# A decoder layer on one core: late gate products 8 chunks later, scatters tied to V blocks, V lists mixed, the branch ahead of the residual

## The chip, the cores and the metric

The kernel runs on one core of a Trainium2 chip. Its engines are named as in the profile: PE (matmuls; PEld are its weight loads), DVE, ACT, POOL and SP; POOL and SP also issue DMAs. The metric is the device time of one execution in microseconds, as the median of several runs. A profiled execution is one execution more, with its own time.

## The reference

One layer of an autoregressive decoder for 256 tokens of 2048 numbers, all in float32: two kinds of attention, an attention into 256 memory tokens, and then a retrieval of experts (PEER), then a last RMSNorm. The change touches only the retrieval and the last norm:

```python
def peer_ffn(hn, w_pq, sub_keys, u_tab, v_tab):          # 8 heads, 16 experts a head, 16384 experts
    q = (xt @ w_pq).reshape(T, PEER_HEADS, 2, PEER_D_KEY // 2)
    s = jnp.einsum('thpd,hpkd->thpk', q, sub_keys)
    top_s, top_i = lax.top_k(s, K)
    ...
    expert = ia * PEER_N_KEYS + ib
    gate = jax.nn.softmax(best_s, axis=-1)
    ...
        a = jnp.einsum('td,ted->te', xb, u_tab[eb])
        hidden = gb.astype(xb.dtype) * jax.nn.gelu(a)
        return jnp.einsum('te,ted->td', hidden, v_tab[eb])
...
h = h + peer_ffn(rmsnorm(h, norm_ffn), ...)
y = rmsnorm(h)
```

## The kernel before

The kernel does not gather rows of U per token. It multiplies the hidden state with the whole of U, 128 chunks of 128 experts each (`u_chunk`), and keeps for each chunk a tile of 128 experts x 256 tokens in one of 16 buffers `hb` of 8 chunks each: 8 in the pool `ba` (chunks 0 to 63), 8 in the pool `bb` (chunks 64 to 127). What no token chose is multiplied by a gate of zero. Then only experts that some token chose are taken further to V.

**Splitting.** Each float32 operand that comes from memory is split in two: `parts` (L66) makes `hi` on ACT (L69) and the remainder `lo` on DVE (L71), in three buffers each; PE multiplies both. A U chunk is two loads of 512 KB (`raw`, SP's queue, four buffers), two splits, 16 matmuls at L79 and 16 at L81 per half. `raw` buffers are also used for late gates and, later, for listed rows.

**Gates.** While the top-k search runs (pieces popped one per chunk), each chosen place gets its gate by an indirect DMA from POOL into a table in DRAM (`put_gate`, L922; 256 of them, four popped per step; `puts`). When all puts have landed, the table is read back. Chunks from `first` on have their gates in their `hb` buffer before their products (eight reads of 1 MB, L730 `hb<-table`). Chunks before `first` were already computed without a gate; groups of four of them are done late (`early`, `done`): one read of 0.5 MB into a `raw` buffer (L730 `gates<-table`), one product on DVE (L702), and a reduction of the largest values (`peaks`, L753). `end` is the chunk at which the last put is popped; reads of late gates begin at `end + 6`.

**Lists.** `lists(part, ...)` (L771) ranks the experts in use and gives each a row in DRAM. There are two parts, experts of chunks 0 to 87 and of 88 to 127, and three classes in each: experts wanted by tokens of the first half only (class 0), of the second half only (class 1), or of both (class 2). One indirect DMA per chunk (L811, "scatter", POOL) writes its rows to their places: 88 in part 0, 40 in part 1. The scatters of part 1 are closures in `late`.

**V blocks.** `plan` cuts the classes into blocks of 128 rows, 22, 22 and 17 in part 0 and 10, 10 and 8 in part 1, 89 blocks in all, and writes their order (`seq`) and the ends of four stretches (`ends`). `block(i)` fetches 128 rows of V for block i + 11 (`fetch`, L963, indirect DMA on POOL, 1 MB, into an `hb` buffer of `ba` or `bb` by the pattern `homes`), reads the listed rows of the block (SP, L1016, up to four blocks at a time into a `raw` buffer), splits the hidden values (`hh` L1003, `hl` L1005) and the V rows, and adds 12 matmuls (24 for class 2) to the four PSUM banks of the token half (L991, L993, L995). `run(n)` does the blocks up to the end of stretch n, and may pop one of `late` per block. `bank(tb)` takes the four PSUM banks of a token half: the second half's only after the first stretch, when the planner's PSUM (`cps`) has been given back.

The order before: stretch 0 is all 22 blocks of class 0 of part 0; stretch 1 mixes classes 1 and 2 of part 0 (39 blocks); stretch 2 classes 0 and 2 of part 1 (18); stretch 3 class 1 of part 1 (10). Between stretch 1 and stretch 2 the residual is added by matmuls with a unit matrix (L1071), and then comes a branch (`rest`, L1132) for experts that found no place; with these inputs its body is skipped. After stretch 2 the first token half is complete, after stretch 3 the second; squares (L1085), products with the gain (L1105, L1123), scaling and stores follow.

**What sets the order.** The framework schedules each engine's instructions ahead of time from a simulated timeline, by priority and readiness, so the order on an engine need not be that of the code; on the chip each engine then runs its list in that order and waits on semaphores. Nothing passes the branch in either direction.

Of the kernel before, what the change touches and what calls it, by code (L numbers as in the profile page):

```python
# [18 lines left out]
F32 = mybir.dt.float32  # L19
F32R = mybir.dt.float32r  # L20
U32 = mybir.dt.uint32
SYNC = mybir.DependencyInfo(mybir.DependencyClass.Sync, mybir.DependencyReason.DATA)
AF = mybir.ActivationFunctionType
ALU = mybir.AluOpType
# [12 lines left out]
GROUP = 8  # L37
# [5 lines left out]
CAPS = ((22, 22, 17), (10, 10, 8))  # L43
# [7 lines left out]
class Layer:  # L51
# [14 lines left out]
    def parts(self, raw, eng=None):  # L66
        nc = self.nc
        hi = self.st.tile([128, HALF], F32R, tag="hi", name="hi", bufs=HI)
        nc.scalar.activation(hi, raw, AF.Copy)  # L69
        lo = self.st.tile([128, HALF], F32R, tag="lo", name="lo", bufs=LO)  # L70
        (eng or nc.vector).tensor_tensor(out=lo, in0=raw, in1=hi.bitcast(F32), op=ALU.subtract)  # L71
        return hi, lo


# [544 lines left out]
    def peer(self):  # L619
        nc, tc, a = self.nc, self.tc, self.a  # L620
        with ExitStack() as es:
# [14 lines left out]
            def some(n):  # L636
                for _ in range(n):
                    if puts:
                        puts.pop(0)()

            with ExitStack() as e2:
                ps = self.ps = e2.enter_context(tc.tile_pool(name="ups", bufs=2, reuse_waits="tile", space=bass.MemoryType.PSUM))
                pieces = []
                with tc.tile_pool(name="tk", bufs=1, reuse_waits="tile") as tk:
# [22 lines left out]
                    c = 0  # L667
# [14 lines left out]
                self.plan()  # L682

                end = c + (len(puts) + 3) // 4
                first = (end + 10 + GROUP - 1) // GROUP * GROUP
                early = list(range(0, first, 4))
                done = {}
                part = 0
                late = []
                while c < 128:  # L690
                    if c % GROUP == 3 and c + 5 >= first and c + 5 < 128:
                        self.table_read(self.buf[(c + 5) // GROUP][:, :, :T], c + 5)
                    if c >= end + 6 and early:
                        g = early.pop(0)
                        t = self.st.tile([128, 4 * W], F32, tag="raw", name="gates", bufs=RAW)
                        t = t[:, :4 * T].rearrange("p (i t) -> p i t", t=T)
                        self.table_read(t, g)
                        done.setdefault(c + 1, []).append((g, t))
                    self.u_chunk(c, c >= first)
                    for g, t in done.pop(c, []):  # L700
                        d = self.buf[g // GROUP][:, g % GROUP:g % GROUP + 4, :T]
                        nc.vector.tensor_mul(d, d, t)  # L702
                        self.peaks(g, g + 4)
                    some(4)
                    if c >= first and (c % 4 == 3 or c >= 124):
                        self.peaks(c if c >= 124 else c - 3, c + 1)
                    c += 1
                    if part == 0 and c >= PARTS[0][1] and not early and not done:
                        late = self.lists(0, ps, "sc", 2)
                        part = 1  # L710
                    if part == 1 and not late and not self.sets:
                        for k in range(11):
                            self.fetch(k)
                    for _ in range(4):
                        if late:
                            late.pop(0)()
# [54 lines left out]
    def lists(self, part, pool, tag, bufs):  # L771


        nc, tc, cl = self.nc, self.tc, self.cl
        lo, hi = PARTS[part]
        n = hi - lo
        v = nc.vector
        cap, base = CAPS[part], BASE[part]
        t = lambda tag, k=2: cl.tile([128, k, n], F32, tag=tag, name=tag)
        f = t("f")  # L780
        v.tensor_scalar(f, self.peak[:, :, lo:hi], 0.0, None, op0=ALU.not_equal)
        both = t("both", 1)
        v.tensor_mul(both[:, 0], f[:, 0], f[:, 1])
        v.tensor_sub(f[:, 0], f[:, 0], both[:, 0])
        v.tensor_sub(f[:, 1], f[:, 1], both[:, 0])
        p = self.ranks(f, n, 2, pool, tag, bufs)
        ok = t("ok")
        for j in range(2):
            v.scalar_tensor_tensor(ok[:, j], p[:, j, :n], float(cap[j] * 128), f[:, j], op0=ALU.is_lt, op1=ALU.mult)
        v.tensor_sub(f, f, ok)  # L790
        for j in range(2):
            v.scalar_tensor_tensor(ok[:, j], p[:, j, :n], float(base[j] - BIG), ok[:, j], op0=ALU.add, op1=ALU.mult)
        for j in range(2):
            v.tensor_add(both[:, 0], both[:, 0], f[:, j])
        p = self.ranks(both, n, 1, pool, tag, bufs)

        limit = float(cap[2] * 128)
        x = t("x", 1)
        v.tensor_scalar(x[:, 0], p[:, 0, :n], limit, ROWS[part] - limit - base[2], op0=ALU.is_ge, op1=ALU.mult)
        v.scalar_tensor_tensor(x[:, 0], p[:, 0, :n], float(base[2] - BIG), x[:, 0], op0=ALU.add, op1=ALU.add)  # L800
        v.tensor_mul(x[:, 0], x[:, 0], both[:, 0])
        for j in range(2):
            v.tensor_add(x[:, 0], x[:, 0], ok[:, j])
        v.tensor_scalar(x[:, 0], x[:, 0], float(BIG), None, op0=ALU.add)
        where = cl.tile([128, n], U32, tag="where", name="where")
        v.tensor_copy(where, x[:, 0])  # L806

        v.tensor_reduce(out=self.over[:, part:part + 1], in_=both[:, 0], axis=AX.X, op=ALU.add)

        def write(i):  # L810
            ins = nc.gpsimd.indirect_dma_start(  # L811
                out=self.rows[part], out_offset=bass.IndirectOffsetOnAxis(ap=where[:, i - lo:i - lo + 1], axis=0),
                in_=self.buf[i // GROUP][:, i % GROUP, :], in_offset=None,
                bounds_check=ROWS[part] + n * 128 - 1, oob_is_err=False)

            tc.declare_no_dep(ins.ins, group="rows%d" % part, reason="rows of their own")
            tc.add_to_no_dep_group("rows%d" % part, ins.ins)
            self.written[part].append(ins)

        return [(lambda i=i: write(i)) for i in range(lo, hi)]  # L820

    def topk_pieces(self, h, tb, pq, sk):
# [108 lines left out]
    def plan(self):  # L931

        self.seq, self.ends, self.sets, self.index = [], [], {}, {}
        self.homes = ([self.ba] * 8 + [self.bb] * 3 + [self.ba] * 8 + [self.bb] * 5) * 4
        for lists in (((0, 0),), ((0, 1), (0, 2)), ((1, 0), (1, 2)), ((1, 1),)):
            todo = []
            for part, cls in lists:
                n = CAPS[part][cls]
                todo += [((k + 0.5) / n, part, cls, k) for k in range(n)]
            self.seq += [x[1:] for x in sorted(todo)]  # L940
            self.ends.append(len(self.seq))

# [26 lines left out]
    def v_phase(self):  # L969
        nc, tc, a = self.nc, self.tc, self.a  # L970
# [5 lines left out]
        with ExitStack() as es:  # L976
            psum = lambda n: tc.tile_pool(name=n, bufs=1, reuse_waits="tile", space=bass.MemoryType.PSUM)
            out = []
# [43 lines left out]
            def block(i):  # L1022
                part, cls, k = self.seq[i]
                if i + 11 < len(self.seq):
                    self.fetch(i + 11)
                raw = self.sets.pop(i)
                listed = load(part, cls, k)
                tbs = (cls,) if cls < 2 else (0, 1)
                for tb in tbs:
                    left[tb] -= 1  # L1030
                h = hidden_pair(listed[:, :T] if cls == 2 else listed[:, cls * 128:(cls + 1) * 128])
                for hf in range(2):
                    vh, vl = self.parts(raw[:, hf * HALF:(hf + 1) * HALF])
                    for tb in tbs:
                        tq = slice(tb * 128, (tb + 1) * 128) if cls == 2 else slice(0, 128)
                        products(tb, hf, [x[:, tq] for x in h], vh, vl, left[tb] == 0)

            at = [0]

            def run(upto, beside=[], after=0):  # L1040


                first = at[0]
                while at[0] < self.ends[upto]:
                    if at[0] - first >= after and beside:
                        beside.pop(0)()
                    block(at[0])
                    at[0] += 1

            bank(0)  # L1050
            with psum("cps") as cps:
                late = self.lists(1, cps, "sc", 2)
# [9 lines left out]
                nc.vector.tensor_copy(self.flag, flag)  # L1062
            nc.gpsimd.dma_start(res, self.hres)
            nc.gpsimd.dma_start(gain, a["norm_final"].partition_broadcast(128))
            run(0, late, 4)
            bank(1)
            run(1, late)

            for tb in range(2):
                for k in range(KD):  # L1070
                    mm(out[tb][k // 4][:, k % 4 * 128:(k % 4 + 1) * 128], res[:, k, tb * 128:(tb + 1) * 128],  # L1071
                       self.ident, start=False, stop=False)
            self.rest(hidden_pair, products)
            run(2)

            one = vw.tile([128, 1], F32, tag="fy", name="one", bufs=2)
# [182 lines left out]
```

## Time and profile before

| | us |
|---|---|
| median of 3 runs | 1842.82 (1840.57 to 1849.99) |
| profiled execution, whole | 1836.41 |
| its span | 1834.6 |
| PE busy / PEld / DVE / ACT / POOL | 1695.8 / 1439.1 / 1272.7 / 961.6 / 760.3 |
| mean granted clock of PE | 0.97 |

The span runs from the first to the last instruction on record; the whole time has 1.8 us around it. Matmuls overlap, so PE's busy time says when PE was not idle rather than how much of its peak was used. In lists of waits the columns are the total, the number and the longest; in the timeline a start, a duration, the engine, and in brackets the idle time before it with what ended it; a duration with `x8` covers eight instructions in a row.

### The profile page before, as it was taken

To read this page: it belongs to the slowest core of one execution; us is meant where nothing else is said; L and a number is where in the kernel's file an instruction comes from. 1 tells how busy PE (TensorE), PEld (TensorE's weight loads), DVE (VectorE), ACT (ScalarE), POOL (GpSimd) and SP (SyncE) were. 2 spreads that over 40 slices of the span, in tenths; PEclk is the share of its full clock that TensorE was granted. 3 is DMA by queue.
4 is the path that set the end of the run, shared out by engine and by line. 5 is a ranking of instruction groups with operands and counts; after the bars stand their busy time and mean duration, and the time that the engine had idled before them with its cause. 6 is when DMAs were issued, how large, how long until landed. Compare 5 with 4: busy or idle time off the path is not lost. (4 is left out here: it accounts for less than half of the span.)

```text
span 1834.6 us, 25771 instructions
## 1 busy us (share of the span) xinstructions
PE 1695.8 (92%) x9056; PEld 1439.1 (78%) x9056; DVE 1272.7 (69%) x2304; ACT 961.6 (52%) x1441; POOL 760.3 (41%) x642
## 2 busy tenths in 40 slices
PE   8899999999999979999997299999999895999897
PEld 6788777887888868888886188888887774888785
DVE  6834575546678999999963299777665793666467
ACT  6534556764565446556543044544443573555356
POOL 5400000112132788888877200004774167744220
PEclk9999999999999989999999599999999997999999
DMA  7566344889846545666663788657888879797551
GB/s 278 170 231 202 134 141 152 317 315 373 277 151 196 174 121 173 184 186 187 192 196 105 247 269 269 205 187 213 253 250 308 319 293 359 299 414 271 203 189 71
DMA packets 127178, 416.30 MB, mean 227 GB/s; under 512 B 38041, under 2 KB 39817, under 8 KB 113344
## 3 DMA queue, kind: packets, MB, share of 16 engines
q1 hardware_dynamic: 88352, 254.34, 42.6%
q0 software_dynamic: 38688, 160.23, 23.9%
q8 instruction: 73, 1.20, 0.3%
q14 instruction: 65, 0.53, 0.1%
HBM read 370.50 MB, written 49.78 MB: 229 GB/s over the span
## 5 line engine op out<-in xcount | busy, mean ns | idle before, releaser
L71 DVE TENSOR_TENSOR lo<-raw,hi 128x1024 fp32r<-128x1024 f32 x436 | 538.3, 1237 | 249.4 <-ACT hi L69 228.6
L69 ACT ACTIVATE hi<-raw 128x1024 fp32r<-128x1024 f32 x440 | 464.5, 1058 | 458.1 <-PE acc L79 208.3
L79 PE MATMUL acc<-pair_f,hi 128*128 128x512 f32 x2304 | 584.7, 396 | 21.9 <-ACT hi L69 8.0
L79 PEld LDWEIGHTS acc<-pair_f,hi 128*128 128x128 f32 x2304 | 418.0, 190 | 100.8 <-ACT hi L69 10.8
L922 POOL DMA_INDIRECT table<-total,place x256 | 339.9, 1328 | 107.9 <-issue 75.2
L81 PEld LDWEIGHTS acc<-pair_f,lo 128*128 128x128 f32 x2304 | 316.7, 192 | 73.4 <-DVE lo L71 51.3
L81 PE MATMUL acc<-pair_f,lo 128*128 128x256 f32 x2304 | 325.2, 284 | 49.4 <-DVE lo L71 49.4
L71 DVE TENSOR_TENSOR lo<-vrows,hi 128x1024 fp32r<-128x1024 f32 x178 | 216.1, 1224 | 120.8 <-ACT hi L69 114.0
L69 ACT ACTIVATE hi<-vrows 128x1024 fp32r<-128x1024 f32 x178 | 186.0, 1059 | 148.2 <-PE out L993 91.1
L963 POOL DMA_INDIRECT vrows<-V,index x89 | 131.7, 1480 | 209.0 <-DVE lo L71 181.7
L811 POOL DMA_INDIRECT rows<-hb,where x128 | 142.3, 1112 | 164.0 <-DVE where L806 125.3
L991 PE MATMUL out<-hi,hh 128*128 128x512 f32 x456 | 140.5, 406 | 29.0 <-ACT hi L69 20.4
L993 PE MATMUL out<-hi,hl 128*128 128x512 f32 x456 | 144.2, 401 | 0.0
L995 PE MATMUL out<-lo,hh 128*128 128x512 f32 x456 | 140.0, 398 | 0.0
L79 PE MATMUL acc<-pair_x,hi 128*128 128x512 f32 x512 | 132.4, 397 | 0.0
L991 PEld LDWEIGHTS out<-hi,hh 128*128 128x128 f32 x456 | 87.0, 193 | 51.0 <-ACT hi L69 21.3
L79 PEld LDWEIGHTS acc<-pair_x,hi 128*128 128x128 f32 x512 | 91.8, 190 | 17.2 <-issue 1.4
L993 PEld LDWEIGHTS out<-hi,hl 128*128 128x128 f32 x456 | 87.1, 191 | 21.4 <-DVE hl L1005 0.2
L995 PEld LDWEIGHTS out<-lo,hh 128*128 128x128 f32 x456 | 86.3, 190 | 20.9
L81 PEld LDWEIGHTS acc<-pair_x,lo 128*128 128x128 f32 x512 | 70.9, 191 | 7.9 <-DVE lo L71 1.9
L81 PE MATMUL acc<-pair_x,lo 128*128 128x256 f32 x512 | 75.2, 286 | 1.5 <-DVE lo L71 1.5
L79 PE MATMUL acc<-pair_o,hi 128*128 128x512 f32 x256 | 66.3, 400 | 5.3 <-ACT hi L69 4.3
(376 smaller groups left out, 1879.1 us busy)
## 6 DMA issues: line engine op xcount, KB each, us to landing
raw<-U SPq DMA_DIRECT2D x256, 512.0 KB, 4.4
raw<-w_sb SPq DMA_DIRECT2D x32, 512.0 KB, 3.4
table<-zero POOLq DMA_DIRECT2D x16, 1024.0 KB, 4.4
raw<-w_out SPq DMA_DIRECT2D x32, 512.0 KB, 6.6
raw<-w_pq SPq DMA_DIRECT2D x32, 512.0 KB, 3.8
rows<-zero POOLq DMA_DIRECT2D x12, 903.0 KB, 9.1
listed<-rows SPq DMA_DIRECT2D x20, 516.0 KB, 4.5
raw<-w_kv SPq DMA_DIRECT2D x16, 512.0 KB, 3.3
```

The lines of the kernel that those rows point to most:

```text
L69: nc.scalar.activation(hi, raw, AF.Copy)
L71: (eng or nc.vector).tensor_tensor(out=lo, in0=raw, in1=hi.bitcast(F32), op=ALU.subtract)
L79: mm(ps, hi[:, n * m:(n + 1) * m], pair[:, k, :], start=first and n == 0, stop=False)
L81: mm(ps[:, T:], lo[:, n * m:(n + 1) * m], pair[:, k, :T], start=False, stop=last and n == len(ks) - 1)
L811: ins = nc.gpsimd.indirect_dma_start(out=self.rows[part], out_offset=bass.IndirectOffsetOnAxis(ap=where[:, i - lo:i - lo + 1], axis=0), in ...
L922: ins = self.nc.gpsimd.indirect_dma_start(out=self.table, out_offset=bass.IndirectOffsetOnAxis(ap=self.place[tb][:, s:s + 1], axis=0), in_ ...
L963: nc.gpsimd.indirect_dma_start(out=raw, out_offset=None, in_=self.a["V"], in_offset=bass.IndirectOffsetOnAxis(ap=self.index[part, cls][:, ...
L991: mm(out[tb][hf * 2 + q], hh, vh[:, q * 512:(q + 1) * 512], start=first, stop=False)
L993: mm(out[tb][hf * 2 + q], hl, vh[:, q * 512:(q + 1) * 512], start=False, stop=False)
L995: ins = mm(out[tb][hf * 2 + q], hh, vl[:, q * 512:(q + 1) * 512], start=False, stop=last)
```

## The change

It consists of five edits.

1. In `peer`: reads of late gates begin at `end + 14` instead of `end + 6`, and `first` is computed from `end + 18` instead of `end + 10`.
2. In `v_phase`: each scatter of part 1 gets a dependency on the last `lo` of the block just written (`self.last_lo`), and is popped after the block instead of before it; the count starts from block 3 instead of 4.
3. In `plan`: stretch 0 is 11 blocks of class 0; stretch 1 mixes the other 11 with classes 1 and 2 (50 blocks); stretch 2 mixes classes 0 and 2 of part 1 with the first 6 of class 1 (24 blocks); stretch 3 is the last 4 of class 1.
4. `bank(1)` thereby comes after 11 blocks.
5. `rest` (the branch) stands ahead of the residual matmuls.

```diff
@@ parts
-        (eng or nc.vector).tensor_tensor(out=lo, ...)
+        self.last_lo = (eng or nc.vector).tensor_tensor(out=lo, ...)
@@ peer
-                first = (end + 10 + GROUP - 1) // GROUP * GROUP
+                first = (end + 18 + GROUP - 1) // GROUP * GROUP
...
-                    if c >= end + 6 and early:
+                    if c >= end + 14 and early:
@@ lists, write(i)
+            return ins
@@ plan
-        for lists in (((0, 0),), ((0, 1), (0, 2)), ((1, 0), (1, 2)), ((1, 1),)):
+        a0, a1, a2 = CAPS[0]
+        b0, b1, b2 = CAPS[1]
+        for lists in (((0, 0, 0, 11),), ((0, 0, 11, a0), (0, 1, 0, a1), (0, 2, 0, a2)),
+                      ((1, 0, 0, b0), (1, 1, 0, b1 - 4), (1, 2, 0, b2)), ((1, 1, b1 - 4, b1),)):
             todo = []
-            for part, cls in lists:
-                n = CAPS[part][cls]
-                todo += [((k + 0.5) / n, part, cls, k) for k in range(n)]
+            for part, cls, lo, hi in lists:
+                todo += [((k + 0.5 - lo) / (hi - lo), part, cls, k) for k in range(lo, hi)]
@@ v_phase, run
                 while at[0] < self.ends[upto]:
+                    block(at[0])
                     if at[0] - first >= after and beside:
-                        beside.pop(0)()
-                    block(at[0])
+                        ins = beside.pop(0)()
+                        tc.add_manual_dep(ins.ins, self.last_lo.ins.name, SYNC, reason="one per block")
                     at[0] += 1
@@ v_phase
-            run(0, late, 4)
+            run(0, late, 3)
             bank(1)
             run(1, late)
+            self.rest(hidden_pair, products)
             for tb in range(2):
                 ... (the residual matmuls)
-            self.rest(hidden_pair, products)
             run(2)
```

More of the change, by code (lines that the diff above doesn't have):

```diff
@@ L70, in parts @@
         lo = self.st.tile([128, HALF], F32R, tag="lo", name="lo", bufs=LO)
-        (eng or nc.vector).tensor_tensor(out=lo, in0=raw, in1=hi.bitcast(F32), op=ALU.subtract)
+        self.last_lo = (eng or nc.vector).tensor_tensor(out=lo, in0=raw, in1=hi.bitcast(F32), op=ALU.subtract)
         return hi, lo
```

## The prediction

> **What bounds the kernel now.** I read first the page (engines and the span in 40 slices), then PE's waits, then the stages in windows, then the timeline around each stop. TensorE is busy 92% of the span, so time can only come from PE's stops; the waits say where they are.
>
> ```profile
> span 1834.6 us, 25771 instructions
> PE   8899999999999979999997299999999895999897
> PEclk9999999999999989999999599999999997999999
> PE acc L81 <- DVE lo L71: 50.8, 4, 48.2
> PE out L991 <- ACT hi L69: 20.4, 2, 14.8
> PE out L991 <- ACT hh L1003: 7.8, 2, 7.1
> ```
>
> The reader is to see two hollows in PE's row (a 2 near slice 23, a 5 near slice 33) and three waits: one of 48.2 us in the U chunks, 20.4 us in two pieces in the V blocks, one of 7.1 us at the branch. Call them A, B and C. All other PE waits are each under 15 us in total and in code that the change leaves alone.
>
> **A, the late gates.**
>
> ```profile
> 985.28 1.11 PE L81 MATMUL acc<-pair_f,lo 128*128 128x256 f32 x8
> 990.87 1.12 PE L81 MATMUL acc<-pair_f,lo 128*128 128x256 f32 x8
> 994.61 2.00 PE L79 MATMUL acc<-pair_f,hi 128*128 128x512 f32 x8
> 1010.87 0.98 POOL L922 DMA_INDIRECT table<-total,place  x1 [0.30 <-issue]
> 1014.13 7.27 POOL L730 DMA_DIRECT2D hb<-table  x8 [2.29 <-issue]
> 1021.39 0.56 POOL L730 DMA_DIRECT2D gates<-table  x1
> 1042.40 1.23 DVE L702 TENSOR_TENSOR hb<-hb,gates 128x1024 f32<-128x1024 f32 x1 [54.55 <-DMA gates<-table]
> 1044.82 2.08 PE L81 MATMUL acc<-pair_f,lo 128*128 128x256 f32 x8 [48.20 <-DVE lo L71]
> 1030.00:1035.00 5.00, 0.00 (x0) 0.00 (x0) 0.00 (x0) 0.00 (x0) 0.00 (x0) 0.50 1.02 351
> 1390.00:1440.00 50.00, 44.87 (x247) 38.04 (x246) 25.18 (x35) 18.55 (x28) 13.33 (x11) 1.00 0.99 397
> ```
>
> (In windows: span, the five engines' busy times, PE's clock, DMA share, GB/s.) One U chunk takes PE 990.87 - 985.28 = 5.59 us. DVE reaches the first late product at 1042.40 - 54.55 = 987.85 and stands; behind it in DVE's order are the splits that feed PE, which runs dry 8.8 us later (994.61 + 2.00 = 996.6). The product waits for a 0.5 MB read that POOL issues at 1021.4, behind its last gate put (1010.9) and eight 1 MB reads; the DMA then moves 351 GB/s and nothing else wants it.
>
> The change puts the product 8 chunks later, 8 x 5.59 = 44.7 us. In numbers of the code: 34 chunks run with the top-k pieces and 72 puts are left, so end = 52, reads start at chunk 66 instead of 58, `first` goes from 64 to 72, the late groups from 16 to 18, the 1 MB reads from 8 to 7. POOL's puts do not wait for DVE there (0.30 us of issue between them), so the reads still start at 1014. What changes is that U loads run beside them: 1.05 MB per 5.59 us is 188 GB/s. The nearest row of such sharing is 1390 to 1440 (V rows beside U loads): 397 GB/s, PE 44.87 of 50, so U got 169 of its 188. From 1014 to 1032.6 U takes 169 and the table reads 351 - 169 = 182 GB/s, 3.4 MB of their 7.9 (7 x 1.05 + 0.52). DVE, 1.9 us late from that sharing, stands at 1034.5; SP still fills four slots (2.1 MB); 4.5 + 2.1 MB at 351 GB/s take 19 us from 1032.6, but the fill is shared, so I put the product at about 1046 to 1051, take 1048. PE resumes 2.4 us after the product (as 1044.82 after 1042.40), at 1050.4, and would have stopped at 1034.5 + 8.8 = 1043.3: about 7 us idle, and 1.9 us of slower chunks. A is worth 48.2 - 7 - 1.9 = 39 us. Bounds: 48 if the reads have landed; and with U at its full 188 GB/s to the end, 7.9 MB at 351 - 188 = 163 GB/s land at 1062, PE idles from 1041 to 1065, worth 25. A loss would need the product after 1042.4 + 44.7 = 1087, excluded by these rates.
>
> The Trainium skill (DMA: Bandwidth & Descriptors, section Queues, rings and completion order) says that each DMA engine goes round robin between queues, a packet at a time. By that the U loads, with 4 KB runs against the table's 1 KB, would lose nothing and the table reads would be the slow ones: the 1.9 us go, the product comes later, and A would be worth about 37; the row of 1390 to 1440, where PE does lose 10% beside larger runs, is no contradiction and no proof.
>
> Extra work in A: two more groups at 1.23 us of product each, eight fewer gated products of 0.42, so nothing in sum; but DVE is nearly full while late products run beside gated chunks, and these overlap now for 10 chunks, not 8.
>
> ```profile
> 1095.00:1140.00 45.00, 44.42 (x253) 38.24 (x253) 43.20 (x62) 20.98 (x31) 3.18 (x6) 1.00 0.81 270
> ```
>
> Here DVE is 43.2 of 45 and PE loses 0.6. I charge 1 us (0 to 3).
>
> **B, the V blocks.**
>
> ```profile
> 1504.76 0.29 ACT L1003 ACTIVATE hh<-listed 128x128 fp32r<-128x128 f32 x1
> 1507.57 0.29 ACT L1003 ACTIVATE hh<-listed 128x128 fp32r<-128x128 f32 x1
> 1493.00:1706.00 213.00, 192.56 (x813) 154.44 (x812) 131.56 (x148) 114.11 (x147) 128.25 (x99) 0.94 0.83 318
> L811 POOL DMA_INDIRECT rows<-hb,where x14 | 15.4, 1102 | 4.3 <-issue 4.0 <-DMA rows<-hb,where 0.3
> 1500.00:1515.00 15.00, 15.00 (x66) 12.06 (x65) 13.71 (x17) 12.00 (x16) 11.65 (x12) 1.00 0.31 94
> 1513.26 1.23 POOL L963 DMA_INDIRECT vrows<-V,index  x1 [0.30 <-issue]
> 1515.00:1550.00 35.00, 14.56 (x52) 11.06 (x51) 10.26 (x13) 9.29 (x14) 27.37 (x26) 0.71 1.00 396
> 1537.52 2.00 ACT L69 ACTIVATE hi<-vrows 128x1024 fp32r<-128x1024 f32 x2 [13.26 <-DMA vrows<-V,index]
> L963 POOL DMA_INDIRECT vrows<-V,index x89 | 131.7, 1480 | 209.0 <-DVE lo L71 181.7 <-issue 9.8 <-DMA index<-rows 4.4
> ```
>
> A block for one half of the tokens is 12 matmuls in 2.81 us (0.234 each), one for both halves 24 in 5.6. From 1493 to 1706 PE did 813 matmuls, 190 us of work in 213: 23 us lost, half-clock matmuls after the stop included. The cause: 14 scatters go through POOL in one run (15.4 + 4.3 us) with no V fetch between them, the DMA falls to 94 GB/s for 15 us, then all fetches come at once, the DMA is full at 396 GB/s, and the row sets of the next blocks land late.
>
> Tied one to a block, a scatter (1.1 + 0.3 us) and a fetch (1.5 + 0.3) take POOL 3.2 us per block. Mixed evenly, the 50 blocks of the second stretch (17 of them double) take PE 187.6 / 50 = 3.75 us each, so POOL keeps up; and 1.05 MB of V plus 0.13 of listed rows per block ask for 315 GB/s, where 22 one-half blocks in a row ask for 420. What waits behind a scatter on POOL is the fetch 12 blocks ahead, which itself waits for a split (181.7 us of `DVE lo` in its row), so the tie's wait costs nothing there. The one tight place is the 24th fetch: its pool `bb` has 8 buffers, 5 of them holding rows of the second part, and its fifth V set needs 16 scatters, the last now tied to block 18. For the prices:
>
> ```profile
> DMA to landing us min/median/max: 2.4/5.3/7.8
> DMA to landing us min/median/max: 5.6/9.4/27.3
> ```
>
> (scatters, then V fetches.) 1.4 + 5.3 + 1.8 + 9.4 = 18 us from block 18's last split to the landed set; PE needs it after blocks 18 to 22, 19.6 us by plan, less about 3.5 us by which that split comes after the block's start: 16. Two us late. B is worth 23 - 2 = 21; bounds 23, and 5 if this fetch takes the longest landing (27.3). Three lists at a time hold three of the four `raw` slots, but by plan each load of listed rows has at least 14.0 us (19.6 before) between the slot's release and its block, against this landing:
>
> ```profile
> listed<-rows SPq DMA_DIRECT2D x20, 516.0 KB, 4.5
> 1483.59 0.19 DVE L800 SCALAR_TENSOR_TENSOR x<-ps_rank,x 128x40 f32<-128x40 f32 x1
> ```
>
> The second PSUM bank is wanted after 11 blocks (about 1493), not 22; the last reader of the planner's PSUM is done at 1483.6, so 9 us cover it.
>
> **C, the branch.**
>
> ```profile
> L1132 ACTq COMPARE_BRANCH  x1: 50/50/50, 1700.0 to 1700.0; - x1
> L1132 PEldq COMPARE_BRANCH  x1: 5267/5267/5267, 1711.1 to 1711.1; - x1
> 1706.21 6.41 PE L1071 MATMUL out<-ident,fin 128*128 128x128 f32 x56
> 1716.53 2.95 ACT L69 ACTIVATE hi<-vrows 128x1024 fp32r<-128x1024 f32 x3 [16.01 <-PEq L1132]
> 1719.73 2.93 PE L991 MATMUL out<-hi,hh 128*128 128x512 f32 x6 [7.10 <-ACT hh L1003]
> 1820.53 2.60 DVE L1105 TENSOR_TENSOR fin<-out,fin 128x512 f32<-128x512 f32 x4
> ```
>
> ACT is at the branch at 1700.0 but goes on only when PE is past it (1716.5); PE then waits 3.2 us more for the first split. With the residual matmuls (56 of 64 in 6.4 us) behind the branch, PE does them while ACT and DVE make that split: the 3.2 us go, the 5.3 us of PE's own branch stay. Bounds 0 and 5. The Trainium skill (Advanced Engine Details and Errata, section Control Flow Timing) gives a compare-and-branch about 108 ns; by that nothing but the 3.2 us would stand here to begin with. PE's row has 5267 ns, and the measurement decides, but the term is the same by both.
>
> The last list is 4 blocks, not 10, so the first half's epilogue has 11 us of matmuls beside it, not 28. Before, its products with the gain start at 1820.5, after the last split, and use none of that cover; 0 (up to 3 us worse).
>
> **Sum.** -39 + 1 - 21 - 3 = -62 us. The profiled execution took 1836.4 us (span 1834.6), so 1774; the runs' median, 1842.8, lies 6.4 above it, so 1781 against that. All best bounds together are -76 (1767), all worst -25 + 3 - 5 - 0 + 3 = -24 (1819).
>
> **The rivals.**
> 1. *A goes only in part* (1794): the table reads lose to the U loads, or the scheduler's order puts the product less than 8 chunks later; it is free to do so, for DVE's order above has it ahead of a split that the code writes earlier. A is then worth about 26. For it: the DMA is full at 1.02 during the reads. Against: the first 18 us of them run before DVE comes.
> 2. *B stays* (1797 to 1802): the 24th fetch or a new run of scatters starves PE again for some 16 to 21 us. For it: the tie lets all scatters whose blocks are done, some 9, go in one run when the list is ready at 1491. Against: the mix leaves POOL and DMA slack to catch up.
> 3. *The steps don't do what they say* (about 1830): the scheduler moves the stop along with the product, so that A and B both remain nearly whole, and only C's 3 us and some of the DMA relief are left.
> 4. *Slower* (about 1950): the tie turns scatter, landing and fetch into one chain on POOL, because each fetch waits for a buffer that the scatter ahead of it must free. Then a block costs 1.1 + 5.3 + 1.5 + 0.6 = 8.5 us against PE's 3.75, 4.8 more for 40 blocks, less the 11 sets fetched ahead (41 us): +150, less A and C (41). It decides against the change from about 19 chained blocks on (41 us of A and C, 9 more to be seen, and the lead of 41, at 4.8 a block). Against it: only the 23rd and 24th fetch need a buffer that scatters free.
>
> **How the numbers follow.** Forecast 0.62 (1781, own range 1770 to 1793), rival 1 0.14, rival 2 0.13, rival 3 0.05, rival 4 0.03, better than the forecast (A whole) 0.03. The range 1766 to 1806 takes in the first three and the best bounds. A measurement here can't tell 0.5% (9 us) from no change; beyond that, faster 0.92 (the first three and the last), same 0.04 and slower 0.04 (rivals 3 and 4 and their neighbours).
>
> **What would show it.** A: DVE's wait for the first late product from 54.5 us to 10 to 18, at chunk 63, the table reads at about 240 GB/s under running matmuls, PE's wait on line 81 below 22 us. B: scatters and fetches alternating on POOL, no 5 us window below 200 GB/s once the mixed blocks run, no PE wait over 5 us between run 0 and the branch. C: the residual matmuls behind the branch, PE idle for 3 to 4 us instead of 7.1. The prediction is wrong if PE's wait in the chunks is still above 25 us, if V sets land late again, or if the four last blocks leave the tail longer than 12 us from PE's last matmul.

## The result and the profile after

The changed kernel takes 1784.97 us (median of 4 runs, 1779.56 to 1787.01), the kernel before 1844.91 beside it (4 runs, 1840.57 to 1849.99): ratio 0.967, 95% interval 0.9635 to 0.9704, about 60 us less. The profiled execution took 1784.79 us with a span of 1782.4; the span before was 1834.6, so the two traces are 52.2 us apart. On the chips of the last eight runs below the kernel before itself took 1893 to 1960 us and the changed kernel was not timed, so the times of those runs decide nothing, and only the order of events in their traces is read.

From the page and from PE's waits (total, number, longest), the lines that answer to those of before:

```profile
span 1782.4 us, 25773 instructions
PE   7899999999998988999999979999999999999997
PEclk9999999999999998999999989999999999999999
PE acc L81 <- DVE lo L71: 18.7, 6, 11.1
PE out L994 <- ACT hi L69: 3.2, 1, 3.2
PE out L1076 <- PEq L1136: 1.9, 1, 1.9
```

The hollows of 2 and 5 in PE's row are gone; what is left of A is a 7 in one slice. A's longest wait went from 48.2 to 11.1 us, B's waits from 20.4 to 3.2, C's from 7.1 to 1.9.

Where the 52.2 us come from is read at landmarks, by the starts of the same work in both traces. In the U chunks the landmark is the last group of products with `lo` of a chunk on PE itself (L81); the joins of a chunk on ACT can trail PE by some us (4 us at chunk 64 before, 16 us after) and don't serve for that. The four rows of each fence are chunks 8, 64, 65 and 116. First before, then after:

```profile
724.05 1.11 PE L81 MATMUL acc<-pair_f,lo 128*128 128x256 f32 x8
1089.24 1.12 PE L81 MATMUL acc<-pair_f,lo 128*128 128x256 f32 x8
1094.83 1.12 PE L81 MATMUL acc<-pair_f,lo 128*128 128x256 f32 x8
1383.24 1.22 PE L81 MATMUL acc<-pair_f,lo 128*128 128x256 f32 x8
```

```profile
726.05 1.12 PE L81 MATMUL acc<-pair_f,lo 128*128 128x256 f32 x8
1040.10 1.11 PE L81 MATMUL acc<-pair_f,lo 128*128 128x256 f32 x8
1058.55 1.12 PE L81 MATMUL acc<-pair_f,lo 128*128 128x256 f32 x8
1354.67 1.21 PE L81 MATMUL acc<-pair_f,lo 128*128 128x256 f32 x8
```

The changed kernel is 2.0 us later at chunk 8 (a hiccup in the first chunks, nothing of the change), 49.1 earlier at chunk 64, only 36.3 at chunk 65, and 28.6 at chunk 116. So the old stop, with what followed it up to chunk 64, was worth 51.1; a new stop takes 12.9 back, and the stretch of late products that follows takes 7.7 more. The first split of a V block stands where chunk 116 left it, 28.7 earlier (first row of each fence below). The last product ahead of the branch is the second row; before, eight residual matmuls (0.9 us) were already done at that point.

```profile
1450.25 1.04 ACT L69 ACTIVATE hi<-vrows 128x1024 fp32r<-128x1024 f32 x1
1705.66 0.72 PE L995 MATMUL out<-lo,hh 128*128 128x512 f32 x2
```

```profile
1421.53 1.06 ACT L69 ACTIVATE hi<-vrows 128x1024 fp32r<-128x1024 f32 x1 [1.43 <-issue]
1658.32 0.63 PE L998 MATMUL out<-lo,hh 128*128 128x512 f32 x2
```

From the one to the other it is 255.2 us before (1705.66 + 0.72 - 0.9 - 1450.25) and 237.4 after: B gave 17.8. The rest, 52.2 - 28.7 - 17.8 = 5.7, is C; the tail from PE's last matmul is 11.8 us and did not change.

The new stop in the chunks, in the timeline after (four rows) and in windows (span, busy time of PE, PEld, DVE, ACT, POOL, PE's clock, DMA share, GB/s):

```profile
1017.91 6.25 POOL L730 DMA_DIRECT2D hb<-table  x7 [3.84 <-DMA table<-total,place]
1031.79 0.56 POOL L730 DMA_DIRECT2D gates<-table  x1 [7.63 <-DVE lo L71]
1051.73 1.23 DVE L702 TENSOR_TENSOR hb<-hb,gates 128x1024 f32<-128x1024 f32 x1 [17.44 <-DMA gates<-table]
1054.15 2.08 PE L81 MATMUL acc<-pair_f,lo 128*128 128x256 f32 x8 [11.09 <-DVE lo L71]
1025.00:1030.00 5.00, 5.00 (x31) 4.46 (x30) 2.89 (x4) 2.19 (x3) 0.00 (x0) 1.00 1.02 378
1050.00:1060.00 10.00, 5.85 (x27) 5.26 (x28) 6.19 (x8) 2.58 (x4) 0.54 (x1) 0.63 0.47 157
1055.00:1165.00 110.00, 103.82 (x574) 89.70 (x574) 97.41 (x135) 49.07 (x73) 8.45 (x16) 0.97 0.74 253
```

DVE stands from 1034.29 to 1051.73 for a read issued at 1031.79, that is 20 us for 0.5 MB behind seven reads of 1 MB. PE runs undisturbed beside these reads (5.00 of 5.00 at 378 GB/s), then idles 11.1 us, and comes back at a clock of 0.63 in the 10 us around the restart: the first 16 products take 4.4 us (1054.15 to 1058.55) where 2.8 are usual. So 11.1 us of waiting cost 12.9. The old stop restarted in the same way (4.5 us for 16, from 1044.82), so its 48.2 us cost 49.9. The last row is the stretch in which late products run between gated chunks: 6.2 us of 110 lost, with two more groups in it than before.

### The profile page after: what moved, and what is told of

It is laid out like the page before. It is cut to its first block, busy times and chain, and to the rows that moved or that the text cites. A ratio compares the mean times of both kernels' runs of the same rounds, so it can differ in the third digit from the quotient of the medians.

```text
span 1782.4 us, 25773 instructions
## 1 busy us (share of the span) xinstructions
PE 1697.2 (95%) x9056; PEld 1440.7 (81%) x9056; DVE 1273.3 (71%) x2298; ACT 962.8 (54%) x1441; POOL 756.1 (42%) x643
## 5 line engine op out<-in xcount | busy, mean ns | idle before, releaser
L81 PEld LDWEIGHTS acc<-pair_f,lo 128*128 128x128 f32 x2304 | 317.0, 193 | 41.9 <-DVE lo L71 20.1
L81 PE MATMUL acc<-pair_f,lo 128*128 128x256 f32 x2304 | 326.2, 285 | 17.3 <-DVE lo L71 17.2
L966 POOL DMA_INDIRECT vrows<-V,index x89 | 125.2, 1407 | 175.1 <-DVE lo L71 147.1
L994 PE MATMUL out<-hi,hh 128*128 128x512 f32 x456 | 134.0, 400 | 5.0 <-ACT hi L69 3.2
L81 PEld LDWEIGHTS acc<-pair_x,lo 128*128 128x128 f32 x512 | 71.2, 192 | 8.0 <-DVE lo L71 1.9
L81 PE MATMUL acc<-pair_x,lo 128*128 128x256 f32 x512 | 75.4, 286 | 1.5 <-DVE lo L71 1.5
```

The costliest lines, as they stand in the source:

```text
L81: mm(ps[:, T:], lo[:, n * m:(n + 1) * m], pair[:, k, :T], start=False, stop=last and n == len(ks) - 1)
L966: nc.gpsimd.indirect_dma_start(out=raw, out_offset=None, in_=self.a["V"], in_offset=bass.IndirectOffsetOnAxis(ap=self.index[part, cls][:, ...
L994: mm(out[tb][hf * 2 + q], hh, vh[:, q * 512:(q + 1) * 512], start=first, stop=False)
```

## The experiments

### One part at a time

Each of these four is the kernel before with one edit of the change, timed beside the kernel before (1840.67 us, median of 16 runs).

**The late gates alone.**

```diff
-                first = (end + 10 + GROUP - 1) // GROUP * GROUP
+                first = (end + 18 + GROUP - 1) // GROUP * GROUP
-                    if c >= end + 6 and early:
+                    if c >= end + 14 and early:
```

> The kernel before with the gate edit alone (first from end + 18, reads from end + 14). Theory (the parts of the change add up): the U chunks end 28 to 31 us earlier than before, as they do in the changed kernel, the stop in the V blocks stays at 15 to 25 us, and the time falls by 26 to 31 us. Rival (the parts need each other, since an earlier start of the V blocks only meets the same scatters and fetches sooner): PE's waits in the V blocks grow by 8 us or more and the time falls by less than 22 us.

Measured: 1801.89 us, ratio 0.9797 (0.9775 to 0.982), 38.8 us less: more than the 26 to 31 of the theory, and not the rival, since the stop in the V blocks stays at 18.2 us. Chunks 8, 64, 65 and 116 on PE in its trace and the stretch of late products; then DVE's waits for late reads in that stretch (1055 to 1165), first here, then in the changed kernel:

```profile
725.56 1.11 PE L81 MATMUL acc<-pair_f,lo 128*128 128x256 f32 x8
1039.61 1.12 PE L81 MATMUL acc<-pair_f,lo 128*128 128x256 f32 x8
1057.99 1.11 PE L81 MATMUL acc<-pair_f,lo 128*128 128x256 f32 x8
1349.08 1.21 PE L81 MATMUL acc<-pair_f,lo 128*128 128x256 f32 x8
1055.00:1160.00 105.00, 102.94 (x576) 90.21 (x576) 99.02 (x138) 49.46 (x73) 8.46 (x16) 0.98 0.81 268
DVE hb L702 <- DMA gates<-table: 5.7, 4, 3.7
DVE hb L702 <- DMA gates<-table: 12.4, 6, 3.0
```

By the same reading the old stop gives 51.1 here too (from +1.5 to -49.6), the new one takes 12.8, as in the changed kernel, but the stretch of late products takes 2.7, not 7.7. The code of that stretch is the same in both kernels. So the stop is a property of the edit; the 5 us between the two traces show as late reads that DVE waits for, 6.7 us longer in the changed kernel, and no run here shows why they land later there.

**The tie alone** (each scatter of part 1 waits for the last `lo` of the block just written, and is popped behind it).

```diff
+                    block(at[0])
                     if at[0] - first >= after and beside:
-                        beside.pop(0)()
-                    block(at[0])
+                        ins = beside.pop(0)()
+                        tc.add_manual_dep(ins.ins, self.last_lo.ins.name, SYNC, reason="one per block")
```

> The kernel before with the tie of the scatters alone; lists, gates and branch as before. Theory A (the hole that the run of scatters tears into the V fetches is the cause): PE's wait for V rows falls from 20.4 us to under 8 and the time by 12 to 20 us. Theory B (22 one-half blocks in a row ask for more than the DMA moves, the scatters only show it): the wait stays above 12 us and the time falls by less than 8 us.

Measured: 1831.78 us, ratio 0.996 (0.9936 to 0.9985), 8.9 us less. That is neither theory: PE's wait for V falls from 20.4 to 12.5 us, not under 8, and the time by a little more than theory B allowed.

**The mix alone** (stretch 0 is 11 blocks, the other 11 of class 0 are mixed with classes 1 and 2, and so on).

```diff
-        for lists in (((0, 0),), ((0, 1), (0, 2)), ((1, 0), (1, 2)), ((1, 1),)):
+        for lists in (((0, 0, 0, 11),), ((0, 0, 11, a0), (0, 1, 0, a1), (0, 2, 0, a2)),
+                      ((1, 0, 0, b0), (1, 1, 0, b1 - 4), (1, 2, 0, b2)), ((1, 1, b1 - 4, b1),)):
```

> The kernel before with the even mix of the lists alone; scatters not tied. Theory A (hole in the fetches): a run of some 14 scatters is still there, and only the slower blocks behind it soften it; the time falls by 5 to 13 us. Theory B (demand of the one-half blocks): the wait goes nearly whole and the time falls by 14 to 20 us, tie or no tie.

Measured: 1833.15 us, ratio 0.9959 (0.9946 to 0.9972), 7.5 us less, as theory A had it.

What the two do is seen on POOL, in groups over the first run of scatters (count, busy, mean ns, idle before), beside the 10 us with the least traffic about that run and PE's wait for V. The tie alone, then the mix alone, then the changed kernel, with the stop that is left there:

```profile
L811 POOL DMA_INDIRECT rows<-hb,where x9 | 10.0, 1114 | 2.7 <-issue 2.4 <-DMA rows<-hb,where 0.3
1500.00:1510.00 10.00, 10.00 (x44) 8.04 (x44) 9.29 (x11) 7.70 (x11) 7.87 (x8) 1.00 0.46 133
PE out L992 <- ACT hi L69: 12.5, 2, 7.6
```

```profile
L811 POOL DMA_INDIRECT rows<-hb,where x14 | 16.1, 1147 | 4.3 <-issue 4.0 <-DMA rows<-hb,where 0.3
1510.00:1520.00 10.00, 10.00 (x45) 8.04 (x44) 6.82 (x9) 5.91 (x9) 7.87 (x8) 1.00 0.26 73
PE out L993 <- ACT hi L69: 12.5, 2, 7.9
```

```profile
L811 POOL DMA_INDIRECT rows<-hb,where x6 | 6.8, 1133 | 1.8 <-issue 1.5 <-DMA vrows<-V,index 0.3
1460.00:1470.00 10.00, 10.00 (x45) 8.04 (x44) 9.35 (x12) 6.86 (x9) 7.87 (x8) 1.00 0.47 182
1510.00:1520.00 10.00, 7.34 (x21) 5.80 (x22) 5.12 (x5) 5.37 (x6) 5.72 (x5) 0.66 1.02 419
1511.55 2.96 ACT L69 ACTIVATE hi<-vrows 128x1024 fp32r<-128x1024 f32 x3 [1.61 <-DMA vrows<-V,index]
```

The tie cuts the run from 14 scatters to 9, since those whose blocks are already done still go at once when the list is ready; PE's wait falls from 20.4 to 12.5. The mix leaves the run of 14 as it is (73 GB/s), but the blocks behind it ask for less V per microsecond (315 against 420 GB/s by the prediction's sum), and the wait falls as much. Together the run is 6 scatters, and one late V set is left (ACT's split at 1511.55 waits for it), for which PE waits 3.2 us. Neither edit does the other's work. Each gain is under 0.5% of the time, so it is the waits in the traces, more than the times, that carry this.

**The branch alone** (`rest` ahead of the residual matmuls).

```diff
+            self.rest(hidden_pair, products)
             for tb in range(2):
                 ...
-            self.rest(hidden_pair, products)
```

> The kernel before with the branch ahead of the residual matmuls alone. Theory: PE's idle time at the branch falls from 7.1 us to 2 to 4 and the time by 3 to 5.5 us. Rival (the residual was cover for the other engines' restart, and ahead of the branch it kept PE's clock up): the residual matmuls run at half clock behind the branch and give back what is gained; the time falls by less than 1.5 us.

Measured: 1832.1 us, ratio 0.9959 (0.9946 to 0.9973), 8.6 us less, more than the 3 to 5.5 of the theory. From the last product ahead of the branch to the end, the trace is 7.1 us shorter than that of before. PE's branch, the last product ahead of it and the residual behind it, here and then in the changed kernel (branch and residual):

```profile
L1132 PEldq COMPARE_BRANCH  x1: 4546/4546/4546, 1704.2 to 1704.2; - x1
1706.68 0.63 PE L995 MATMUL out<-lo,hh 128*128 128x512 f32 x2
1708.96 7.38 PE L1072 MATMUL out<-ident,fin 128*128 128x128 f32 x64 [1.65 <-PEq L1132]
```

```profile
L1136 PEldq COMPARE_BRANCH  x1: 3826/3826/3826, 1656.8 to 1656.8; - x1
1660.81 9.01 PE L1076 MATMUL out<-ident,fin 128*128 128x128 f32 x64 [1.86 <-PEq L1136]
```

PE's queue reaches the branch at 1704.2, 3.1 us before the last product ends (1706.68 + 0.63), so of 4.5 us of branch 1.65 are seen; before, it reached it at 1711.1, 1.5 us before the last residual matmul ended (1706.21 + 6.41), and 7.1 us were seen: 3.8 to the end of the branch, 3.3 to the first split behind it. The four single gains are 38.8 + 8.9 + 7.5 + 8.6 = 63.8; the whole change gave 59.9.

### What is left of the stops

These eight ran in two groups of four. The kernel before took 1931.64 us beside the first group (median of 13 runs) and 1941.55 us beside the second (9 runs). Where a kernel ran twice, once in each group, expectations and times stand in that order; the later gates ran in the first group, the two edits together in the second.

**The changed kernel with each 1 MB read bound to the subtraction of the chunk before**, twice.

```diff
-                        self.table_read(self.buf[(c + 5) // GROUP][:, :, :T], c + 5)
+                        ins = self.table_read(self.buf[(c + 5) // GROUP][:, :, :T], c + 5)
+                        tc.add_manual_dep(ins.ins, self.last_lo.ins.name, SYNC, reason="not ahead of the late gates")
```

> The changed kernel, with each of the seven 1 MB reads of the table tied to the last split of the chunk before it, so that they no longer stand ahead of the late gates. Theory (what is left of the stop in the chunks is the late read standing behind 7 MB): DVE waits for the first late product 0 to 4 us instead of 17.4, PE's wait of 11.1 us goes, and the time is 10 to 17 us below the changed kernel's. Rival (the read is late because its buffer is free only at 1031.8): DVE still waits over 8 us and the time falls by less than 6 us.

> The changed kernel with each of the seven 1 MB reads of the table bound to the subtraction of the chunk before, so that they no longer stand in the queues ahead of the first late gate read. Theory (the first late product waits because its small read shares the queues with seven reads of 1 MB): VectorE's wait of 17.4 us for the first late product falls under 6 us, TensorE's stop of 11.1 us goes, and with the ramps about it 10 to 16 us of the time: 1769 to 1776 us. Rival (the small read is slow by itself, or beside the U loads): the wait stays over 14 us and the time at 1782 to 1788 us. Rival (the 1 MB reads, now late, are missed by the chunks that use their gates): new waits of VectorE for hb<-table, 1790 us or more.

Measured: 1907.67 us; 1873.16 us (ratio 0.983, 0.9742 to 0.9918, against the kernel before).

**Late gates still later** (the changed kernel with reads of late gates from `end + 17`).

```diff
-                    if c >= end + 14 and early:
+                    if c >= end + 17 and early:
```

> The changed kernel, with reads of late gates from end + 17 instead of end + 14 and first as it is. Theory (the stop is the read's landing at 1051 against DVE's coming): DVE comes 17 us later, the stop falls from 11.1 us to under 2, but three more late products run beside gated chunks; the time is 6 to 14 us below the changed kernel's if the slow chunks behind the stop come from the reads of the table landing late, and within 4 us of it if they come from DVE being full where late products and gated products overlap (13 chunks instead of 10).

Measured: 1925.15 us.

**Two scatters behind each of the first V blocks**, twice.

```diff
-                    if at[0] - first >= after and beside:
-                        ins = beside.pop(0)()
-                        ...
+                    for _ in range(2 if len(beside) > 24 else 1):
+                        if at[0] - first >= after and beside:
+                            ins = beside.pop(0)()
+                            ...
```

> The changed kernel, with two scatters per block in blocks 3 to 10 and one in each after them. Theory (PE's 3.2 us wait at block 23 is the V fetch that needs 16 scatters): the 16th scatter is done some 20 us earlier, the wait and the half-clock matmuls behind it go, and the time is 2 to 6 us below the changed kernel's. Rival (a longer run of scatters tears a hole into the fetches, as before): a wait for V rows of over 5 us, and the time is 2 us or more above.

> The changed kernel with two scatters instead of one behind each V block until 24 are left. Theory (the 24th fetch waits for sixteen scatters that come one to a block, and so lands 3 us late): the stop at blocks 23 and 24 (3.2 us and as much again at a lower clock) goes, 3 to 5 us: 1777 to 1782 us. Rival (two scatters between fetches make the fetches before them late, with single stops over 3 us before block 20): 1783 to 1790 us.

Measured: 1913.8 us, and 1914.28 us (ratio 0.9932, 0.9754 to 1.0111).

**The bound reads and the two scatters together** (both diffs in one kernel).

> Both edits together: the bound 1 MB reads, and two scatters behind each of the first V blocks. If the two stops are apart in time and cause, their gains add up: 13 to 20 us, 1764 to 1772 us. Where one of the two theories falls, the other's gain alone: 1769 to 1782 us.

Measured: 1925.72 us, ratio 1.008 (0.9997 to 1.0162).

**Mix and tie together, on the kernel before**, twice (the two diffs above).

> The kernel before with tie and mix, without the gate edit and the branch. Theory (the two do what they did in the changed kernel): PE's wait for V rows falls from 20.4 us to about 3 to 5 and the time by 16 to 20 us. Rival (part of that came from the other edits): less than 13 us.

> The kernel before with the tied scatters and the even mix together, without the other two parts. Alone they gave 8.9 and 7.5 us. If they take away different stops, 15 to 18 us: 1823 to 1826 us. If each needs the other (a tied scatter comes one to a block, and the old mix needs more of them), more than the sum, 19 to 23 us: 1818 to 1822 us. If both remove the same wait, 9 to 11 us: 1830 to 1832 us.

Measured: 1913.89 us, and 1919.64 us (ratio 0.9972, 0.98 to 1.0144).

No expected time can be judged by these. In all eight traces PE's chunks ran late, by 53 to 100 us of pauses for which the profile shows no cause, while POOL's reads did not wait for them. That answers two questions. The first is why the first late read takes 20 us. In the kernel with two scatters, whose late gates are those of the changed kernel, the seven reads of 1 MB go at 1025.76 and the first late read only at 1084.17, when the DMA is half idle (last row):

```profile
1025.76 6.25 POOL L730 DMA_DIRECT2D hb<-table  x7 [1.75 <-DMA table<-total,place]
1084.17 0.56 POOL L730 DMA_DIRECT2D gates<-table  x1 [52.16 <-DVE lo L71]
1087.93 1.23 DVE L702 TENSOR_TENSOR hb<-hb,gates 128x1024 f32<-128x1024 f32 x1 [1.26 <-DMA gates<-table]
1080.00:1085.00 5.00, 5.00 (x31) 4.42 (x30) 3.06 (x4) 2.11 (x4) 0.56 (x1) 1.00 0.52 184
```

Issue to product is 3.8 us beside running U loads, and there is no stop. In the second mix and tie run, whose gates are those of before, the first late read goes 23 us after the first of the eight 1 MB reads, with the DMA still full (last row), and takes 16.4:

```profile
1033.71 7.28 POOL L730 DMA_DIRECT2D hb<-table  x8 [2.28 <-issue]
1056.64 0.56 POOL L730 DMA_DIRECT2D gates<-table  x1 [15.65 <-DVE lo L71]
1073.02 1.23 DVE L702 TENSOR_TENSOR hb<-hb,gates 128x1024 f32<-128x1024 f32 x1 [13.80 <-DMA gates<-table]
1065.00:1070.00 5.00, 0.00 (x0) 0.00 (x0) 0.00 (x0) 0.18 (x1) 0.00 (x0) 0.90 1.03 358
```

The first run of that same kernel, on another chip, is the best control: there the read goes 44 us after the first 1 MB read and takes 4.2. So the same read takes 3.8 to 4.2 us when it comes long after the 1 MB reads, or ahead of them where they are bound (seven of the eight traces), and 16 to 21 us while the DMA is still full with them (19.9 after, 20.0 with the late gates alone, 21.0 before). The remaining stop comes from the large reads ahead, and neither from the product nor from the read itself. With the 1 MB reads bound, DVE waits 1.3 to 1.5 us for its first late read and never for a 1 MB read; but with the reads unbound or later it waits 1.3 to 1.4 on those chips too, so these traces don't show that binding them, or reading the late gates still later, takes away the 12.9 us.

The second question is the stop around V blocks 23 and 24. With two scatters a block the first run is 12 scatters instead of 6, and PE waits 4.3 us in one run and 2.7 in the other for a late V set, where it waited 3.2 (9.8 in two pieces with the bound reads added). The rows are of the first run:

```profile
L811 POOL DMA_INDIRECT rows<-hb,where x12 | 14.2, 1186 | 3.7 <-issue 3.7
PE out L994 <- ACT hi L69: 4.3, 1, 4.3
```

The stop did not go. The idea that only the sixteenth scatter is late falls with it: it is issued 28 us ahead of the split that waits, against 15 in the changed kernel. In the 20 us ahead of that split the DMA is nearly full in both (387 to 422 GB/s); that it is the demand which makes the set late is likely, and not shown.

The mix and tie traces also bear on the sum of the two edits. Without the other parts of the change PE waits 5.9 and 5.5 us for V, against 12.5 with either alone and 20.4 before. The chips differ, but the direction is that of the changed kernel (3.2): each edit takes away its own part.

## Why the prediction was right, and where its steps were off

The time came out 4 us above the forecast of 1781, inside the range. The mechanisms were right; that the number came so near is in part luck. A sum of -62 against the profile stands beside 52.2 between the traces. Of the 10 us, 6 do not show in the medians, because the profiled execution of before lay 6.4 us below its median, while that of after (1784.79) lies on its median. The forecast added the 6.4 as if it would stay. The traces of the tie, the mix and the branch alone, which leave the gates as they were, show where some of it lay: their wait in the chunks is 50.7 to 50.8 us, not 48.2.

**A, forecast -38 with the extra DVE work; between the traces -30.6 without the 2 us of the first chunks.** The mechanism and the place were right: the product came 8 chunks later, between the joins of chunks 62 and 63, and the table reads had some 234 GB/s (7.9 MB from 1017.9 to 1051.7; forecast about 240), most of the time under running matmuls. Three terms were mis-sized. The largest is the extra work in the stretch of late products, charged 1 us (0 to 3): it took 7.7 here and 2.7 with the gates alone. The prediction counted DVE's work there; what came on top were late reads that DVE waited for, 12.4 us here and 5.7 with the gates alone. The remaining stop was taken as 7 us idle; PE waited 11.1. The product came 3.7 us later than the 1048 assumed, since the 1 MB reads went only at 1017.9, not 1014, after the puts had landed. And the 1.9 us of slower chunks did not exist: without the start's 2.0 us, DVE came to the product 44.4 us later than before, against 44.7 for eight chunks. That DVE stood from 1034.3, where 1034.5 was forecast, is luck, the start's 2.0 in the place of those 1.9. The slow clock behind the stop was not charged either, but it cost 1.6 us behind the new stop and 1.7 behind the old one, so leaving it out of both did no harm.

That agrees with what the prediction worked out from the Trainium skill (DMA: Bandwidth & Descriptors, section Queues, rings and completion order), by which each DMA engine goes round robin between queues, a packet at a time: the U loads, with the larger runs, held their pace, PE was busy 5.00 of 5.00 us at 378 GB/s in all, and the waits alone fell by 37.1 (48.2 - 11.1), where it gave about 37. The traces do not show the packets themselves. The nearest row that the sum used instead (V rows beside U loads, 44.87 of 50) was no measure of this sharing; in the changed kernel the same work, 28.6 us earlier, still loses 3.3 of 50 at 394 GB/s:

```profile
1361.00:1411.00 50.00, 46.66 (x252) 40.10 (x251) 27.11 (x39) 19.68 (x29) 11.53 (x9) 0.96 0.97 394
```

**B, forecast -21; 17.8.** The cause was right and both halves of the edit were needed, as the single runs show. The remaining stop, charged 2 us, was the mis-sized term: it cost 3.2 of waiting and 2.6 of slow products behind it (14 in 5.9 us from 1512.66, where 3.3 are usual; a clock of 0.66 in the window about it). Of the signs named, scatters and fetches alternate after the first run and no wait over 5 us is left. The tight place was named (the 24th fetch) and the only stop stands there, but the reason given, its sixteenth scatter, is not borne out by the runs with two scatters a block; so far that was luck. Windows below 200 GB/s do occur: 182 over the first run of 6 scatters (56 in its second 5 us) and 28 from 1600 to 1610 while POOL waits, and PE loses nothing in the first and 0.4 us in the 10 us after the second; that sign was too strict. A slip of the sum: with the longest landing of 27.3 the fetch comes 20 us late, so the worst bound of B is 3, not 5, and that of the whole 1821.

**C, forecast -3 (0 to 5); -5.7 in the change, and 7.1 in the trace of the run alone.** The step that failed is "the 5.3 us of PE's own branch stay". By the prediction's own rows only 3.8 of them were seen (from 1712.62, the end of the residual, to 1716.4). They stay only in part: PE's queue comes to a branch ahead of the matmuls still running, and what runs out meanwhile covers it, 3.1 us in the run with the branch alone against 1.5 before. PE's visible stop became 1.9 where the forecast said 3 to 4. The branch also was shorter (3826 and 4546 ns against 5267); why is not shown. In the run alone no slow clock is seen in the residual behind it (7.38 us for 64), while before, the first six products after the stop took 2.93 us, twice their usual 0.23 each. In the changed kernel the residual itself ran slow (9.01 us), 1.6 us more, which is about what the gain there is smaller by. The Trainium skill's figure for a compare-and-branch, about 108 ns (Advanced Engine Details and Errata, section Control Flow Timing), is not what any of these traces has for PE.

**The rivals.** Rival 1 was half right: A went in part, 30.6 where the forecast had 38 and the rival 26, but with the U loads undisturbed and the product at its chunk, so by a longer wait and the stretch behind it. Rival 2 did not come, though its sign did: the ready blocks' scatters went in one run, 6 instead of 9. Rivals 3 and 4 did not come: the stops went with the order of the code, and the tied scatters waited for DVE 9 times and 7.8 us in all.

## What to carry to other kernels

A stop that waits for data costs its idle time and a slow restart: here 1.6 to 1.7 us behind stops of 11.1 and 48.2 us, and 0 to 2.6 behind stops of 1.7 to 3.2. So the restart hardly matters for a long stop and can nearly double a short one. To see what a stop cost, compare the work of the engine that must not stop; joins on another engine trailed it here by 4 and 16 us. A small read that something waits for should not be issued behind large ones that nobody needs yet: it lands when they land. To keep a queue's fetches flowing, both the burst in front of them and the demand behind them count; easing either alone took away 7.9 of the 20.4 us of waiting, and both together 17.2.

## What the runs showed of the hardware

- The same 0.5 MB read took 3.8 to 4.2 us to its product when it came 44 us or more after the 1 MB reads or ahead of them, and 16 to 21 us while the DMA was still full with seven or eight of them, even 23 us after the first of these.
- PE lost nothing while U loads ran beside 1 MB table reads at 378 GB/s in all, while U loads beside V rows cost PE 5 of 50 us at 397 (ACT waited for the U loads there).
- A branch on PE took 3.8 to 5.3 us in three traces, on ACT, DVE, SP and POOL 50 to 72 ns, and ran under matmuls already in PE's queue.
- The granted clock was 0.63 in the 10 us around the end of an 11.1 us stop and 0.66 around one of 3.2 us.
